# Retention of a hybrid layer in a hand-written order, one stream of weights, step sizes in eleven pieces, tiles at 64-byte starts

## The chip, the core and the metric

One core of one Trainium2 chip runs the whole layer as one program. The metric is the device time of one execution in microseconds (us). The kernel before takes 1260.97 us, the median of three executions (1256.4 to 1261.17).

## The reference: what is computed

A layer with 512 latent tokens, 256 context tokens and a model width of 1024 runs two branches side by side: retention (4 heads, keys of 256, values of 512) and a state-space scan (32 heads in 8 groups, state 128, chunks of 64 tokens). Both go forward and backward over the tokens, with the context first. A gated merge and a norm close the layer. Everything is float32.

```python
h_l = rmsnorm(x, norm_pre) * (1 + scale_l) + shift_l      # latent; h_c for the context
q, k, v, g, z, xbc, dt, gt = split(h @ w_in)              # both sequences
# retention, per head and direction: y_t = q_t h_t,  h_t = gamma h_{t-1} + k_t v_t^T
yr = bidir_scan(q, k, v, log_gamma)
# scan: depthwise conv of width 5 and silu on xbc -> xs, B, C; dt = softplus(dt + bias)
ys = bidir_scan(C, B, xs * dt, dt * A)
yr = (yr - mean(yr)) * rsqrt(var(yr) + EPS) * ret_gn_w    # per head
o_ret = (yr * silu(g)) @ w_ret_o
ys = groupnorm((ys + D * xs) * silu(z))
o_ssd = (ys * ssd_norm_w) @ w_ssd_o
out = (sigmoid(g_r) * o_ret + sigmoid(g_s) * o_ssd) @ w_out
x_new = x + gate * rmsnorm(out, norm_post)
```

## The kernel before, in words

Matmuls run on the fp32r type. To keep float32 accuracy each operand is split into a high part (`hh`, `whi`, `qh`, `vh`, `ah`) and a rest (`hl`, `wlo`, `ql`, `vl`, `al`), and each product takes three matmuls: high by high, high by rest, rest by high (`mm3`, L139 to L146; `v_unit`, L183 to L192). The high part is a cast on ScalarE and the rest a subtraction on VectorE. Weights come in units of 128 by 1024 values: a DMA into `wraw`, the cast (L134) and the subtraction (L135), with three buffers of each (`wunit`, L127).

The program has five stages.

1. Prologue, 0 to 60 us: the norm, the modulation, transposes of x, and head 0's q and k. It stands in an order written out by hand (`tc.manual_schedule()`), in which every engine takes its instructions as they are written.
2. Retention, 60 to 495 us, loop `for h in range(4)`: `strip` makes the decay table of a head (L579 to L585); `attention` (L588 to L617) does six steps of scores, decay, split and values: `a` is scores by decay on VectorE (L598), `ah` its cast on ScalarE (L162), `al` its rest on VectorE (L163), and then 12 matmuls into four accumulators (L608 to L610); `gproj` makes the gate (four weight units, L633); `norm` normalises the result into `yn` (L619); `qkv` makes the next head's q, k, v (eight weight units); `finish` (L645) turns `yn` with 16 transposes (L648), multiplies it with the gate into `u` (L650) and stores `u` in DRAM (L651). Apart from head 0's q, k and v, no order is written for this stage: a scheduler sets it when the program is built, from its own estimates.
3. `stepsizes` (L654 to L778), which the scan needs later, is written in the same loop as two pieces, the first behind head 1's q, k and v: a projection (L671), the softplus (`log1p_exp`, L167), sums along the tokens (L699 and L703), exponentials (L727 to L742), and eleven small DMAs that put the rows into DRAM and fetch a table back (L757 to L761); the second, behind head 2's q, k and v, is nine transposes and their copies (L766 to L776).
4. Scan, 495 to 1000 us: again an order by hand (`slot`), one weight unit to a slot.
5. Tail, 1000 to 1260 us: the output projections (L144 to L146 on `uh`, `ul`, and L1329) in the scheduler's order.

Tiles come from pools that place them one behind the other at 32-byte steps, from the left or from the right end of a partition. `vt` takes 1160 bytes, `nhalf` 4, `osq` 16, and so on, so that some pools' tiles start on a multiple of 64 bytes and others 32 bytes past one. On a multiple of 64 start `hh`, `hl`, the three buffers each of `wraw`, `whi` and `wlo`, all large tiles of retention, and, in the tail, the pool `f1` (it holds six of the eight pairs `uh`, `ul` of the second output projection). 32 bytes past one start the prologue's `xt`, `xn`, `wmod` and its fourth weight unit, the scan's `rows`, `x2`, `c2`, `st`, `vw`, `xtok`, `btok`, and, in the tail, the pools `fp` and `f2`: all eight pairs `uh`, `ul` of the first output projection, the other two of the second, and the operand `mg` of the last product (L1329).

Of the kernel before, what the change touches and what calls it, by code (L numbers as in the profile page):

```python
# [63 lines left out]

@with_exitstack
def hybrid_layer_kernel(ctx: ExitStack, tc: tile.TileContext, x, xc, vec, tab, msk, w_mod, bgate, npost,
# [4 lines left out]
    cp = ctx.enter_context(tc.tile_pool(name="cp", bufs=1))  # L71
    wp = ctx.enter_context(tc.tile_pool(name="wp", bufs=3))
# [51 lines left out]
    hp = hstack.enter_context(tc.tile_pool(name="hp", bufs=1))  # L124
# [57 lines left out]

    def v_unit(pv, u, wu, tiles=range(6)):  # L183
# [12 lines left out]
    with ExitStack() as st:  # L196
        p0 = st.enter_context(tc.tile_pool(name="p0", bufs=1))
        pw = st.enter_context(tc.tile_pool(name="pw", bufs=4))
        px = st.enter_context(tc.tile_pool(name="px", bufs=6))
        p2 = st.enter_context(tc.tile_pool(name="p2", bufs=2))  # L200
# [24 lines left out]
        srcs = [w_q[0], w_q[1], w_k[0], w_k[1]]  # L225
# [9 lines left out]
        def load_w(c):  # L235
            wraw[c] = (wp if c < 3 else p0).tile([P, UNIT], F32, name="wraw", tag="wraw")
            nc.sync.dma_start(wraw[c], srcs[c])
# [160 lines left out]
        vraw, vws = [], []  # L398

        def load_v():  # L400
            vraw.append(wp.tile([P, UNIT], F32, name="wraw", tag="wraw"))
            nc.sync.dma_start(vraw[-1], w_v[0, len(vraw) - 1])

        def cast_v():
            hi = wp.tile([P, UNIT], F32R, name="whi", tag="whi")
            nc.scalar.copy(hi, vraw[len(vws)])
            vws.append([hi])

        def rest_v():
            w, raw = vws[-1], vraw[len(vws) - 1]  # L410
            w.append(wp.tile([P, UNIT], F32R, name="wlo", tag="wlo"))
            nc.vector.tensor_tensor(w[1], raw, w[0].bitcast(F32), ALU.subtract)

        for _ in range(3):
            load_v()
        context = {5: (0,), 6: (1, 2)}
        select(3)
        for k in range(2, KT):
            acc(0, k)
            if k + 1 < KT:  # L420
                modulate(k + 1, context.get(k, ()))
            else:

                cast_v()
                head(3, 1)
                head(4, 1)
                rest_v()
                tail(3, 1)
                tail(4, 1)
# [22 lines left out]
        v_unit(first_v, 0, vws[0], range(2))  # L452
# [8 lines left out]
    with ExitStack() as st:  # L461
        rc = st.enter_context(tc.tile_pool(name="rc", bufs=1, reuse_waits="tile"))
        r1 = st.enter_context(tc.tile_pool(name="r1", bufs=1, reuse_waits="tile"))
        r2 = st.enter_context(tc.tile_pool(name="r2", bufs=2, reuse_waits="tile"))
# [64 lines left out]
        def first_qkv():  # L529
# [6 lines left out]
            load_v()  # L536
            read = [rope_read(accs[2 + c], c, *k_dst(c)[:2]) for c in range(2)]
            cast_v()
            rest_v()
# [6 lines left out]
            pv = first_v + [bank2() for _ in range(4)]  # L546
            for u in range(4):
                v_unit(pv, u, vws[u], range(6) if u else range(2, 6))
                if u < 2:
                    cast_v()  # L550
                    rest_v()
                if u == 1:
# [4 lines left out]
        def qkv(h):  # L557
            for c in range(2):
                ps = bank()
                proj(ps, projw(wunit(w_q[h * 2 + c])), 0, LT)  # L560
                rope(ps, c, q_dst(c))
            for c in range(2):
                wk = projw(wunit(w_k[h * 2 + c]))
# [3 lines left out]
                proj(pc, wk, LT, LC)  # L567
                rope(ps, c, k_dst(c))
                split(kh[:, c, LT:], kl[:, c, LT:], pc)

            pv = [bank() for _ in range(2)] + [bank2() for _ in range(4)]
            for u in range(4):
                v_unit(pv, u, wunit(w_v[h, u]))
            for i in range(6):
                split(vh[:, i, :], vl[:, i, :], pv[i])

        def strip(h):
# [8 lines left out]
            return e1, ec  # L586
# [46 lines left out]
        def gproj(h):  # L633
            g2 = big["g2"]
            for d in range(4):
                wk = projw(wunit(w_g[h * 4 + d]))
                ps = bank()
                proj(ps, wk, 0, LT)
                th = r2.tile([P, LT], F32, name="gth", tag="sw")
                nc.scalar.activation(th, ps, AF.Tanh, scale=0.5)  # L640
                nc.vector.scalar_tensor_tensor(g2[:, d, :], th, 1.0, ps, ALU.add, ALU.mult)
            return g2

        def finish(h, yn, g2):
            for d in range(4):  # L645
                ps = bank()
                for j in range(4):
                    nc.tensor.transpose(ps[:, j * P:(j + 1) * P], yn[:, j, d * P:(d + 1) * P], ident)  # L648
                u = r2.tile([P, LT], F32, name="u", tag="t1")
                nc.vector.scalar_tensor_tensor(u, ps, col(V_GN + h * 4 + d), g2[:, d, :], ALU.mult, ALU.mult)  # L650
                nc.sync.dma_start(u_d[0][h * 4 + d], u)  # L651

        def stepsizes():

            sp = st.enter_context(tc.tile_pool(name="sp", bufs=1))
            t = lambda n, w=384: sp.tile([P, w], F32, name=n, tag=n)

            raw = wp.tile([P, UNIT], F32, name="wraw", tag="wraw")
            nc.sync.dma_start(raw, w_dt)
            both = wp.tile([P, UNIT], F32R, name="whi", tag="whi")  # L660
# [146 lines left out]
        for h in range(4):  # L807
# [4 lines left out]
            if h < 3:  # L812
                qkv(h + 1)
# [645 lines left out]
```

## Time and profile before

| | |
|---|---|
| median of three executions | 1260.97 us |
| the profiled execution, its own time | 1262.49 us |
| its span, first to last instruction | 1260.7 us |
| mean granted TensorE clock | 0.994 of full speed |
| TensorE matmul (PE) busy | 1232.9 us, 6539 matmuls |
| VectorE (DVE), ScalarE (ACT), GpSimd (POOL) busy | 820.3, 440.4, 323.6 us |

PE's busy time comes from matmuls that overlap in the pipeline: one of 128 x 512 is recorded with 0.39 us, and the next one starts 0.227 us after it. How fast PE goes is therefore read from the distance of starts, or from the count of matmuls in a stretch, and lost time from gaps between starts.

### The profile page before, as it was taken

The page shows a single profiled execution, that of the slowest core. Times are in us where ns is not written, and L with a number is a line of the kernel's source. Part 1 is how long each engine was busy: PE and PEld are TensorE (multiplying, and loading weights), DVE is VectorE, ACT ScalarE, POOL GpSimd, SP SyncE. Part 2 cuts the span into 40 slices and gives each one's busy share as a digit, 9 for nine tenths or more (in the row PEclk, how much of TensorE's full clock was granted, in tenths as well). Part 3 has the DMA queues.
Part 4 walks back from the last instruction along what each step waited for, and adds up shares of the span by engine and source line. Part 5 has one row for each costly group of instructions (what it writes and reads, how often), then busy time and mean ns, then how long its engine had stood idle before and what let it go on. Part 6 is the DMA issues. An engine that isn't in the chain of part 4 may idle for free.

```text
span 1260.7 us, 16364 instructions
## 1 busy us (share of the span) xinstructions
PE 1232.9 (98%) x6539; PEld 1020.5 (81%) x6539; DVE 820.3 (65%) x971; ACT 440.4 (35%) x702; POOL 323.6 (26%) x267
## 2 busy tenths in 40 slices
PE   8999999899999999999999999999999999999997
PEld 6688887688888888888888888888878888888876
DVE  5576434853454253979999999999993357254533
ACT  4452323233323212444444434444442443122221
POOL 0021010001011000375565757565572200000000
PEclk9999999899999999999999999999999999999999
DMA  9330212122202214325253342515343567344621
GB/s 373 123 108 32 84 68 92 21 85 67 84 34 84 67 51 147 146 67 201 64 204 120 148 184 84 201 51 217 115 154 101 174 192 224 112 149 153 215 84 67
DMA packets 43101, 155.94 MB, mean 124 GB/s; under 512 B 5097, under 2 KB 5897, under 8 KB 37906
## 3 DMA queue, kind: packets, MB, share of 16 engines
q1 hardware_dynamic: 42322, 152.77, 34.8%
q0 software_dynamic: 704, 2.13, 0.7%
q8 instruction: 51, 0.84, 0.3%
q14 instruction: 24, 0.20, 0.0%
HBM read 144.10 MB, written 10.78 MB: 123 GB/s over the span
## 4 chain that ended last, share of the span: by engine, by line
PE 83%; DVE 12%; issue 3%; ACT 1%; DMA 1%; DVEq 0%; SPq 0%; POOLq 0%; ACTq 0%
PE pj L144 11%; PE pj L145 11%; PE pj L146 11%; PE pr L144 7%; PE pb L191 7%; PE pr L146 7%; PE pr L145 7%; PE pj L191 3%; PE py L1058 3%; DVE wlo L800 2%; PE pj L1329 2%; PE pb L1329 2%; PE tk L1005 2%; DVE cacc L887 2%; PE pb L610 2%
## 5 line engine op out<-in xcount | busy, mean ns | idle before, releaser
L144 PE MATMUL pr<-hh,whi 128*128 128x512 f32 (+1 forms) x640 | 240.9, 376 | 0.0
L146 PE MATMUL pr<-hh,wlo 128*128 128x512 f32 (+1 forms) x640 | 229.4, 358 | 0.0
L145 PE MATMUL pr<-hl,whi 128*128 128x512 f32 (+1 forms) x640 | 229.3, 358 | 0.0
L135 DVE TENSOR_TENSOR wlo<-wraw,whi 128x1024 fp32r<-128x1024 f32 x80 | 97.9, 1224 | 151.1 <-ACT whi L134 148.5
L134 ACT CAST whi<-wraw 128x1024 fp32r<-128x1024 f32 x80 | 84.3, 1053 | 229.9 <-PE pj L145 156.3
L144 PEld LDWEIGHTS pr<-hh,whi 128*128 128x128 f32 x640 | 121.0, 189 | 21.0 <-issue 4.6
L145 PEld LDWEIGHTS pr<-hl,whi 128*128 128x128 f32 x640 | 121.1, 189 | 18.1 <-issue 1.9
L146 PEld LDWEIGHTS pr<-hh,wlo 128*128 128x128 f32 x640 | 120.9, 189 | 18.0
L144 PE MATMUL pj<-hh,whi 128*128 128x512 f32 (+1 forms) x352 | 130.6, 371 | 0.0
L145 PE MATMUL pj<-hl,whi 128*128 128x512 f32 (+1 forms) x352 | 130.4, 370 | 0.0
L146 PE MATMUL pj<-hh,wlo 128*128 128x512 f32 (+1 forms) x352 | 130.4, 370 | 0.0
L1027 POOL TENSOR_TENSOR rows<-rows,ctok 128x512 f32<-128x512 f32 x64 | 92.3, 1467 | 104.8 <-DMA rows<-rows_d 104.8
L1044 POOL TENSOR_TENSOR rows<-c,rows 128x512 f32<-128x512 f32 x64 | 116.0, 1838 | 0.0
L800 DVE TENSOR_TENSOR wlo<-wraw,whi 128x1024 fp32r<-128x1024 f32 x56 | 91.5, 1633 | 20.9 <-ACT whi L793 20.9
L146 PE MATMUL pj<-uh,wlo 128*128 128x512 f32 x256 | 101.2, 395 | 0.0
L145 PE MATMUL pj<-ul,whi 128*128 128x512 f32 x256 | 100.8, 394 | 0.0
L144 PE MATMUL pj<-uh,whi 128*128 128x512 f32 x256 | 100.4, 392 | 0.0
L887 DVE SCALAR_TENSOR_TENSOR cacc<-raw,vt,cacc 128x772 f32<-128x772 f32 x48 | 74.8, 1559 | 14.6 <-ACT cacc L885 13.7
L896 ACT ACTIVATE cth<-cacc 128x772 f32<-128x772 f32 (+1 forms) x32 | 25.5, 796 | 145.1 <-DVE cacc L892 145.1
L144 PEld LDWEIGHTS pj<-hh,whi 128*128 128x128 f32 x352 | 66.3, 188 | 11.7 <-issue 0.2
L145 PEld LDWEIGHTS pj<-hl,whi 128*128 128x128 f32 x352 | 66.4, 189 | 11.3
L146 PEld LDWEIGHTS pj<-hh,wlo 128*128 128x128 f32 x352 | 66.3, 188 | 11.3
(303 smaller groups left out, 2316.8 us busy)
## 6 DMA issues: line engine op xcount, KB each, us to landing
rows<-rows_d SPq DMA_DIRECT2D x32, 1024.0 KB, 7.5
wmod<-in_w_mod_dram SPq DMA_DIRECT2D x8, 1024.0 KB, 10.9
wraw<-in_w_v_dram SPq DMA_DIRECT2D x16, 512.0 KB, 3.4
wraw<-in_w_g_dram SPq DMA_DIRECT2D x16, 512.0 KB
wraw<-in_w_xs_dram SPq DMA_DIRECT2D x16, 512.0 KB, 3.6
wraw<-in_w_z_dram SPq DMA_DIRECT2D x16, 512.0 KB, 3.4
wraw<-in_w_gt_dram SPq DMA_DIRECT2D x16, 512.0 KB, 4.6
uraw<-u_d SPq DMA_DIRECT2D x32, 256.0 KB, 3.7
```

The source lines that it names most:

```text
L134: nc.scalar.copy(hi, raw)
L135: (eng or nc.vector).tensor_tensor(lo, raw, hi.bitcast(F32), ALU.subtract)
L144: nc.tensor.matmul(ps, ah, bh, start=(first and i == 0), stop=False)
L145: nc.tensor.matmul(ps, ah, bl, start=False, stop=False)
L146: nc.tensor.matmul(ps, al, bh, start=False, stop=(last and i == n - 1))
L191: nc.tensor.matmul(pv[i], a[:, k, sl], wv[b][:, k2, :], start=(k == 0 and j == 0), stop=(k == KT - 1 and j == 2))
L800: nc.vector.tensor_tensor(lo, r, hi.bitcast(F32), ALU.subtract)
L887: nc.vector.scalar_tensor_tensor(acc, raw[:, i:i + n], col(w0 + i), acc, ALU.mult, ALU.add)
L1027: nc.gpsimd.tensor_tensor(v64(rows[:, d, :]), v64(rows[:, d, :]), bc(cb, 3, 64), ALU.add)
L1044: nc.gpsimd.tensor_tensor(rows[:, 2 + d, :], self.c2, rows[:, 2 + d, :], ALU.mult)
L1058: nc.tensor.matmul(py[64 * q:64 * q + 64, sl], lhs, rhs, start=(term == 0), stop=(term == 2))
L1329: nc.tensor.matmul(pss[e], mg[k][a][:, sl], wo[k][b][:, ec], start=(k == 0 and j == 0), stop=(k == KT - 1 and j == 2))
```

## The change

It has four parts.

- Retention is put under the hand-written order: `order.close()` moves from the end of the first q, k and v to the end of the scan, so that prologue, retention and scan are one order. The loop over heads is written out for it: `attention`, `norm`, then four gate units (`gate(d)`), with a quarter of the old `finish` (`turned(h, d)`, four transposes, one `u`, one store) behind the second, third and fourth unit and the last behind the first q unit; `strip(h + 1)` stands behind the first gate unit.
- All weight units from head 0's values to the scan's gates stand in one list `srcs`. `ahead()` casts and splits the unit two ahead, and `rest` loads the one three further.
- `stepsizes` gets nine more `yield`s: its first stage is eleven pieces, the first behind head 0's gate and the others one each behind a value unit or a gate unit (`step()`); its last, the nine transposes, stands at the end of head 3.
- `Lines` wraps the pools: a tile whose row isn't a multiple of 64 bytes is rounded up to one, `x2` rows get 784 instead of 772 values, and a tile `edge` of 32 bytes at the right end shifts everything that is placed from there.

What each engine computes is the same, instruction by instruction.

```diff
+class Lines:
+    def tile(self, shape, dt, **kw):
...
+        if n % 16 == 0:
+            return self.pool.tile(shape, dt, **kw)
+        t = self.pool.tile([shape[0], -(-n // 16) * 16], dt, **kw)[:, :n]
+        return t if len(shape) == 2 else t.rearrange("p (a b) -> p a b", a=shape[1])
...
-    cp = ctx.enter_context(tc.tile_pool(name="cp", bufs=1))
+    cp = Lines(ctx.enter_context(tc.tile_pool(name="cp", bufs=1)))
+    edge = ctx.enter_context(tc.tile_pool(name="edge", bufs=1, side="right"))
+    edge.tile([P, 8], F32, name="edge", tag="edge")
...
+    srcs = [w_v[0, u] for u in range(4)]
+    for h in range(4):
+        srcs += [w_g[h * 4 + d] for d in range(4)]
+        if h == 0:
+            srcs.append(w_dt)
+        if h < 3:
+            srcs += [w[h * 2 + 2 + c] for w in (w_q, w_k) for c in range(2)] + [w_v[h + 1, u] for u in range(4)]
...
+        def ahead():
+            cast(at[0] + 1)
+            rest(at[0] + 1)
+
+        def values(pv, first=False):
             for u in range(4):
-                v_unit(pv, u, vws[u], range(6) if u else range(2, 6))
...
+                v_unit(pv, u, unit(), range(2, 6) if first and u == 0 else range(6))
+                ahead()
+                if first and u == 1:
                     log_decays()
+                    strip(0)
+                if u < 3:
+                    step()
             for i in range(6):
                 split(vh[:, i, :], vl[:, i, :], pv[i])
...
-        def finish(h, yn, g2):
-            for d in range(4):
...
+        def turned(h, d):
+            ps = bank()
+            for j in range(4):
+                nc.tensor.transpose(ps[:, j * P:(j + 1) * P], big["yn"][:, j, d * P:(d + 1) * P], ident)
+            u = r2.tile([P, LT], F32, name="u", tag="t1")
+            nc.vector.scalar_tensor_tensor(u, ps, col(V_GN + h * 4 + d), big["g2"][:, d, :], ALU.mult, ALU.mult)
+            nc.sync.dma_start(u_d[0][h * 4 + d], u)
...
         first_qkv()
-        order.close()
-        steps = stepsizes()
         for h in range(4):
-            e1, ec = strip(h)
-            py = attention(h, e1, ec)
-            g2 = gproj(h)
-            yn = norm(py)
-            if h < 3:
-                qkv(h + 1)
-            if h < 2:
-                next(steps)
...
-            finish(h, yn, g2)
+            py = attention(h, stripe, ecs)
+            norm(py)
+            gate(0)
+            if h < 3:
+                strip(h + 1)
+            gate(1)
+            turned(h, 0)
+            step()
+            gate(2)
+            turned(h, 1)
+            step()
+            gate(3)
+            step()
+            if h == 0:
+                pieces[0] = 1
+                next(steps)
+            if h < 3:
+                turned(h, 2)
+                qkv(lambda: turned(h, 3))
+            else:
+                next(steps)
+                turned(h, 2)
+                turned(h, 3)
...
+        prev.early()
+        order.close()
```

How the instructions move shows best on VectorE where head 1's attention opens. Of before, from the first of the four `u` to the first score product (`dtu`, `dts`, `dt` belong to the step sizes, `wlo` is a weight's rest, `a` the scores by the decay):

```order
L650 SCALAR_TENSOR_TENSOR u<-pj,vt,g_706 128x512
L676 TENSOR_TENSOR dtu<-dtu,dtm 128x384
L650 SCALAR_TENSOR_TENSOR u<-pj,vt,g_706 128x512
L680 TENSOR_SCALAR dtu<-dtu,vt 128x384
L135 TENSOR_TENSOR wlo<-wraw,whi 128x1024
L169 TENSOR_SCALAR dts_1713<-dte 128x384
L650 SCALAR_TENSOR_TENSOR u<-pj,vt,g_706 128x512
L170 RECIPROCAL dts<-dts_1713 128x384
L650 SCALAR_TENSOR_TENSOR u<-pj,vt,g_706 128x512
L171 TENSOR_TENSOR dts<-dts,dte 128x384
L598 TENSOR_TENSOR a<-pj,strip 128x512
```

Of the change, the same place: the end of the step sizes' softplus, the last weights' rests, the six splits of the values, and the first score product:

```order
L196 TENSOR_SCALAR dt<-dt 128x384
L244 TENSOR_TENSOR wlo<-wraw,whi 128x1024
L740 TENSOR_TENSOR dt<-dt,dtu 128x384
L743 TENSOR_SCALAR dta<-dta 128x1
L745 TENSOR_SCALAR dtu<-dt,dta 128x384
L244 TENSOR_TENSOR wlo<-wraw,whi 128x1024
L182 TENSOR_TENSOR vl<-pj,vh 128x512 x2
L182 TENSOR_TENSOR vl<-pb,vh 128x512 x4
L661 TENSOR_TENSOR a<-pj,strip 128x512
L182 TENSOR_TENSOR al<-a,ah 128x512
```

The `u` and the step sizes no longer stand between the values' splits and the scores; they come before, among the projections.

On TensorE, before, head 0's 16 transposes stood together, between the step sizes' projection and head 1's scores:

```order
L671 MATMUL pj<-hh,whi 128x256
L671 MATMUL pj<-hl,whi 128x256
L648 MATMUL pj<-ident,yn 128x128 x16
L144 MATMUL pj<-qh,kh 128x512
L145 MATMUL pj<-ql,kh 128x512
```

Of the change, head 0's second group of four, between the third and the fourth gate unit (`whi`, `wlo` of the gate's weights):

```order
L164 MATMUL pj<-hl,whi 128x512
L165 MATMUL pj<-hh,wlo 128x512
L700 MATMUL pj<-ident,yn 128x128 x4
L163 MATMUL pj<-hh,whi 128x512
```

Each group of four now has a weight unit of 24 matmuls before it and, but for head 3's last two, one behind it. In prologue, scan and tail every engine keeps its order, but for one weight load that SyncE issues earlier at the prologue's end.

## Rows read from the trace of the kernel before

**Rows 1.** The page, part 1: busy us of each engine (share) xinstructions.

```profile
PE 1232.9 (98%) x6539; PEld 1020.5 (81%) x6539; DVE 820.3 (65%) x971; ACT 440.4 (35%) x702; POOL 323.6 (26%) x267
```

**Rows 2.** Windows, PE: start:end us, length, busy (xmatmuls), clock, DMA share, GB/s.

```profile
213.00:253.00 40.00, 32.20 (x119) 0.87 0.18 50
...
1035.00:1115.00 80.00, 80.00 (x345) 1.00 0.51 161
1122.00:1202.00 80.00, 80.00 (x351) 1.00 0.53 173
```

**Rows 3.** Waits of PE: engine line <- releaser: us in total, times, longest us.

```profile
PE pb L608 <- ACT ah L162: 4.6, 1, 4.6
PE tk L1005 <- DVE vw L990: 4.3, 7, 1.7
...
PE pj L648 <- DVE g L641: 1.2, 1, 1.2
```

**Rows 4.** Timeline, PE: start us, us, engine, line, operation, [idle before <-releaser].

```profile
217.61 0.50 PE L144 MATMUL pj<-qh,kh 128*128 128x512 f32 x1 [1.88 <-DVE u L650]
...
220.64 0.79 PE L144 MATMUL pj<-qh,kh 128*128 128x512 f32 x1 [0.87 <-DVE u L650]
221.23 0.63 PE L145 MATMUL pj<-ql,kh 128*128 128x512 f32 x1
221.66 0.63 PE L146 MATMUL pj<-qh,kl 128*128 128x512 f32 x1
...
248.57 0.51 PE L608 MATMUL pb<-vh,ah 128*128 128x512 f32 x1 [4.55 <-ACT ah L162]
...
340.91 0.98 PE L610 MATMUL pb<-vh,al 128*128 128x512 f32 x3 [0.84 <-DVE al L163]
```

**Rows 5.** Timeline, DVE, at the opening of head 1's attention.

```profile
217.47 2.54 DVE L170 RECIPROCAL dts<-dts 128x384 f32<-128x384 f32 x1
...
220.97 0.68 DVE L598 TENSOR_TENSOR a<-pj,strip 128x512 f32<-128x512 f32 x1
```

**Rows 6.** Timeline, DVE and ACT, at the opening of head 0's attention.

```profile
100.39 0.69 DVE L598 TENSOR_TENSOR a<-pj,strip 128x512 f32<-128x512 f32 x1
...
101.00 1.22 DVE L135 TENSOR_TENSOR wlo<-wraw,whi 128x1024 fp32r<-128x1024 f32 x1
...
101.12 0.62 ACT L162 CAST ah<-a 128x512 fp32r<-128x512 f32 x1 [0.56 <-DVE a L598]
...
102.13 0.69 DVE L163 TENSOR_TENSOR al<-a,ah 128x512 fp32r<-128x512 f32 x1
```

**Rows 7.** Chain of waits, a run of transposes: start us, us, what, count.

```profile
332.86 0.98 PE pj L766 x9
```

**Rows 8.** Groups by line, DVE, 205 to 262 us: busy us, mean ns.

```profile
L175 DVE SCALAR_TENSOR_TENSOR dt<-dt,dts 128x384 f32<-128x384 f32 x7 | 3.8, 549 | 0.0
...
L699 DVE TENSOR_TENSOR_SCAN cum<-dtm,dtu 32x384 f32<-32x384 f32 x2 | 1.9, 947 | 0.1
```

**Rows 9.** Tile tot_d: SyncE's issue, ns min/median/max; landing time of its DMAs.

```profile
L760 SPq DMA_DIRECT2D tot_d<-et x1: 582/582/582, 246.2 to 246.2; - x1
...
DMA to landing us min/median/max: 2.7/2.7/2.7
```

**Rows 10.** Chain of waits, runs of 128 x 512 matmuls.

```profile
77.22 5.44 PE pb L191 x24
...
1209.08 22.35 PE pb L1329 x96
1231.43 22.38 PE pj L1329 x96
```

**Rows 11.** Line L163: duration ns min/median/max, first and last start us.

```profile
L163 DVE TENSOR_TENSOR ul<-uraw,uh x40: 673/692/694, 992.3 to 1212.4; 128x512 fp32r<-128x512 f32 x40
...
L163 DVE TENSOR_TENSOR al<-a,ah x24: 678/692/1671, 102.1 to 465.8; 128x512 fp32r<-128x512 f32 x24
```

**Rows 12.** Window, all engines, the scan.

```profile
500.00:950.00 450.00, 445.54 (x2792) 376.05 (x2792) 419.25 (x390) 191.90 (x335) 267.12 (x190) 1.00 0.39 142
```

More of the change, by code (lines that the diff above doesn't have):

```diff
@@ L397, in hybrid_layer_kernel @@
         nc.sync.dma_start(tb, tab[:, 0:T_ID])
[L398 to L415, printed above, removed]
+        for t in range(3):
+            load(t)
         context = {5: (0,), 6: (1, 2)}
@@ L422, in hybrid_layer_kernel @@
             else:
-                cast_v()
+                cast(0)
                 head(3, 1)
                 head(4, 1)
-                rest_v()
+                rest(0)
                 tail(3, 1)
@@ L451, in hybrid_layer_kernel @@
         first_v = [bank(i=i) for i in (2, 3)]
-        v_unit(first_v, 0, vws[0], range(2))
+        v_unit(first_v, 0, wks[0], range(2))
         first_k = []
@@ L535, in first_qkv @@
                 rope_rest(read[c][0], *q_dst(c)[2:])
-            load_v()
             read = [rope_read(accs[2 + c], c, *k_dst(c)[:2]) for c in range(2)]
-            cast_v()
-            rest_v()
+            cast(1)
+            rest(1)
             for c in range(2):
@@ L567, in qkv @@
                 proj(pc, wk, LT, LC)
+                ahead()
                 rope(ps, c, k_dst(c))
                 split(kh[:, c, LT:], kl[:, c, LT:], pc)
[L571 to L575, printed above, removed]
+            values([bank() for _ in range(2)] + [bank2() for _ in range(4)])
         def strip(h):
@@ L653, in stepsizes, with gate @@
+        def gate(d):
+            ps = bank()
+            proj(ps, projw(unit()), 0, LT)
+            ahead()
+            th = r2.tile([P, LT], F32, name="gth", tag="sw")
+            nc.scalar.activation(th, ps, AF.Tanh, scale=0.5)
+            nc.vector.scalar_tensor_tensor(big["g2"][:, d, :], th, 1.0, ps, ALU.add, ALU.mult)
         def stepsizes():
-            sp = st.enter_context(tc.tile_pool(name="sp", bufs=1))
+            sp = Lines(st.enter_context(tc.tile_pool(name="sp", bufs=1)))
@@ L665, in stepsizes @@
+            ahead()
             u = t("dtu")
@@ new lines, in hybrid_layer_kernel @@
+        for i in range(4):
+            fetch(i)
+        jobs, dst = group_jobs(0)
+        prev = old = cur = None
+        t = scan0
+        for g in range(-1, 8):
+            nxt = Scan(g + 1, *dst) if g < 7 else None
+            for s, job in enumerate(jobs):
+                held = prev if g == 7 and s == 1 else None
+                if held:
+                    prev = Late(prev)
+                slot(s, t, job, prev, old, cur, nxt)
+                if held:
+                    sbx.close()
+                    fr = Lines(fstack.enter_context(tc.tile_pool(name="fr", bufs=1, side="right", reuse_waits="tile")))
+                    gr = fr.tile([P, KT, LT], F32, name="gr", tag="gr")
+                    for d in range(KT):
+                        jobs[d].dst = gr[:, d, :]
+                    held.early()
+                prev = job
+                t += 1
+            old, cur = cur, nxt
+            if g < 6:
+                jobs, dst = group_jobs(g + 2)
+            else:
+                jobs = [Gate(w_gt[d], None, False) for d in range(KT)]
```

195 lines of the change are left out of this document (87 added, 108 removed).

## The prediction

> **What bounds the kernel now.** I read the page first: TensorE's matmul row is busy for 98% of the span, and no other engine for more than 65% [rows 1]. So the chain that sets the end runs through PE, and time can come from two places only: gaps between matmuls, and matmuls that follow each other more slowly than they could. The busy figure shows neither, since a matmul of 512 columns is recorded with 0.39 us while its follower starts sooner. So next I read counts. Where nothing disturbs, 24 matmuls take 5.44 us, which is 0.2267 us each [rows 10]; this is the pace that everything below is held against.
>
> For the gaps I went to the windows of PE and to its waits. In the 40 us from 213 to 253 only 119 matmuls begin, at a mean granted clock of 0.87 [rows 2]; at the pace it would be 176. So 57 x 0.2267 = 13.0 us are lost there. The timeline shows three things in it [rows 4]: two waits of 1.88 and 0.87 us for `u`, one of 4.55 us for `ah`, and, behind the idle stretches, matmuls 0.43 us apart (221.23 to 221.66) instead of 0.23. [...] DVE's timeline shows why `u` and `ah` are late: the step sizes' reciprocal of 2.54 us starts at 217.47 among the four `u`, and the first `a` of the attention only at 220.97 [rows 5]. Two smaller gaps follow: 0.84 us for `al` at head 2 [rows 4] and 1.2 us in which head 3's transposes wait for a gate [rows 3]. Everything else of retention runs at the pace.
>
> **The change, part by part.**
>
> *The old gaps.* With the fixed order, no `u` and no step-size operation stands between the values' splits and the attention's products. The 13.0 us go, and with them the low clock, since PE no longer stands idle before those matmuls. The two small gaps go too: 13.0 + 0.8 + 1.2 = **15.0 us**.
>
> *What the fixed order costs instead.* At the opening of each attention PE has only two score blocks (12 matmuls, 2.72 us) ahead of the first product. In head 0, which has this order already but for one `wlo` of 1.22 us, `a` starts at 100.39, `ah` ends at 101.74 [rows 6]. PE is through its scores by about then. Without the `wlo`, `al` would follow at once and end 0.69 us later, at 102.43; the order now wants it as third matmul, at 101.74 + 2 x 0.2267 = 102.19. That is 0.24 us a head, **1.0 us** for four; the bounds are nothing (the scheduler's order hid it) and 0.84 us a head, the row of head 2 [rows 4], 3.4 in all. In the later steps the same chain, 0.69 + 0.62 + 0.69 = 2.0 us, runs beside the step before it, 12 matmuls or 2.72 us, and is covered. At head 3's end the third `u` needs the bank of the last gate, whose cast and product take about as long as one `ah` and one `a`, 1.3 us [rows 6], against nine transposes of 0.98 us that stand between [rows 7]: **0.4 us**, from nothing to the 1.2 of the row that it replaces [rows 3]. Twelve more groups of transposes change no count; the bound is a switch of 0.1 us each, 1.2 in all, and I take nothing, since the nine at 332.86 follow fp32r matmuls and still take 0.109 us each [rows 7].
>
> *The step sizes in eleven pieces* keep their instructions; I cost them at nothing, because of what covers them. The longest piece is the softplus: one reciprocal of 2.54 [rows 5] and 13 operations of at most 0.55 [rows 8], under 9.7 us on DVE. It stands behind a value unit of 36 matmuls, 8.2 us of PE, and DVE also owes that unit's `wlo` of 1.22 us. DVE falls behind by some 3 us. It may: the rests are made two units ahead, and the next pieces (the sums, two pairs of 0.95 us [rows 8], and shorter ones) are smaller than their units. Without that lead it would cost those 3 us once. Their eleven DMAs pass SyncE's queue behind head 2's second gate, at 0.58 us or less each, plus one wait of 2.7 us for a landing [rows 9], at most 9 us. Weight loads queue behind them, but each is issued three units, 16 us, before its cast. If that lead were gone the price would be those 9 us, once. The loads, stores and POOL's work are spread, not added.
>
> *Tiles at 64-byte starts.* In the tail, 384 matmuls of the first output projection stream tiles that start 32 bytes past a 64-byte line, and they go at 80/345 = 0.2319 us [rows 2]; in the second, where twelve of sixteen operands start on a line, it is 80/351 = 0.2279 us [rows 2]; the last 192 matmuls have one operand on a line and one off it, and take (22.35 + 22.38)/192 = 0.2330 us [rows 10]. PE is not waiting in any of them. Brought to the pace, this is 384 x 0.0052 + 384 x 0.0012 + 192 x 0.0063 = 2.0 + 0.5 + 1.2 = **3.7 us**. Bounds: nothing, if something else in the tail slows them, and 4.5 with the prologue's one such weight unit and rounding of the counts. [...] I follow the rows, because two projections of the same code, in the same stage, differ in nothing that I can see but the starts of their operands. For DVE I take nothing: the subtraction of 128 x 512 takes 692 ns on `uraw`, off the line, and 692 ns on `a`, on it [rows 11].
>
> *The sum*: 15.0 - 1.0 - 0.4 + 3.7 = 17.3 us less. The profiled execution's own time, 1262.49 us, becomes 1245.2. It stood 1.5 us above the median of the three runs, so the median is forecast at **1243.5 us**. About 0.5%, 6 us, is what a measurement of this kernel can tell from no change.
>
> **The rivals.**
>
> *The starts give nothing* (0.12). The tail's slow pace would then come from its traffic: its DMAs are busy at 0.51 and 0.53 [rows 2]. Against it, the two stretches have the same traffic and different paces. Time: 1243.5 + 3.7 = 1247.
>
> *The scan moves as well* (0.11). There DVE is busy 419 of 450 us, and PE waits for it 4.3 us in all at `vw` [rows 12, 3]. A scan that starts in another phase, or with `rows`, `st` and `x2` on a line, may lose or double these waits: 1239 or 1248.
>
> *The gaps only move* (0.06): the change doesn't do what it says, PE meets 13.6 us of new waits in the order by hand, and only the starts count: 1260.97 - 3.7 = 1257. Head 0's opening, in this order and without such gaps, speaks against it [rows 6].
>
> *Slower* (0.03). Each of the 24 attention steps has those 2.72 us of cover for its chain of 2.0 us. If POOL's work falls into that chain, `a` and `al` grow: the longest `al` is 1671 ns against 692 [rows 11]. With 0.98 us more for both, the chain is 4.0 us and PE waits 1.2 us a step, 24 x 1.2 = 30: 1273. It decides from 0.7 us of added time a step. [...] Against the rival: the new order gives POOL nothing to do during attention.
>
> **How the numbers follow.** The forecast has 0.68, with its own range of 1239 to 1247 from the bounds of its small terms. The range 1237 to 1251 takes in the starts and the scan, and the upper bounds of the openings. Faster by over 0.5% (below 1254.7): 0.68 + 0.12 + 0.11 = 0.91; within: 0.06; slower: 0.03.
>
> **What would show it.** Right: no stretch of retention with a clock below 1.0; projections and values at 0.227 us a matmul without gaps; PE's waits for `u` gone, four waits for `al` of some 0.25 us; both output projections and the last product at 0.227 us; the scan as long as before. Wrong: PE waiting for a `wlo` in head 1's values, or for `al` by over 1 us a head, or the tail still at 0.232.

## The result, and the profile after

The changed kernel takes 1244.86 us (median of four executions, 1244.13 to 1246.43); the kernel before, run beside it, 1259.43. The ratio is 0.989, with a 95% interval of 0.986 to 0.991. The profiled execution took 1245.43 us, its span is 1243.7. The forecast was 1243.5 with a range of 1237 to 1251, and on the profiled execution's scale 1245.2. By the medians the change gives 14.6 us. By the two profiled executions, from which the account below is cut, it gives 17.1, since the profiled execution of the kernel before, 1262.49, lies 3.1 us above its median.

The page of the kernel after, parts 1 and 4 (the busy shares, and who holds the chain that ended last):

```profile
PE 1224.3 (98%) x6539; PEld 1016.3 (82%) x6539; DVE 817.1 (66%) x971; ACT 439.4 (35%) x702; POOL 327.6 (26%) x267
...
PE 91%; DVE 6%; issue 2%; ACT 1%; DMA 1%; SPq 0%; DVEq 0%; POOLq 0%; ACTq 0%
```

PE's 98% is what it was [rows 1], which once more tells nothing. The windows tell it (start:end, length, PE busy (xmatmuls), clock, DMA share, GB/s):

```profile
212.00:252.00 40.00, 39.92 (x177) 1.00 0.04 14
1020.00:1100.00 80.00, 80.00 (x355) 1.00 0.53 163
1107.00:1187.00 80.00, 80.00 (x355) 1.00 0.55 182
```

Against [rows 2]: at head 1's opening 177 matmuls begin where there were 119, at the full clock; both output projections show 355 in 80 us, where there were 345 and 351. PE's waits (engine line <- releaser: us in total, times, longest), of which the two for `u` [rows 4] and the long one for `ah` [rows 3] are gone:

```profile
PE tk L1059 <- DVE vw L1044: 5.1, 6, 3.1
...
PE pj L700 <- DVE g L711: 0.4, 1, 0.4
```

The first of these grew, from 4.3 in all and 1.7 at most [rows 3]. Cutting the span at the starts of named matmuls (the first scores of head 0, the scan's first projection, each tail product) gives the account:

| stage, us | before | after | difference | forecast |
|---|---|---|---|---|
| start and prologue | 98.82 | 97.37 | -1.45 | 0 |
| retention | 395.68 | 383.07 | -12.61 | -13.6 |
| scan, with the gates behind it | 534.99 | 536.77 | +1.78 | 0 |
| first output projection | 89.61 | 87.04 | -2.57 | -2.0 |
| second output projection | 89.42 | 88.35 | -1.07 | -0.5 |
| last product | 44.88 | 43.74 | -1.14 | -1.2 |
| behind PE's last matmul | 7.32 | 7.32 | 0 | 0 |
| span | 1260.72 | 1243.66 | -17.06 | -17.3 |

The sum fits better than its terms, and that is luck. Retention gave 1.0 less than forecast, the tail 1.1 more, and a prologue and a scan that the change hardly touches moved by -1.5 and +1.8. The prologue's move is within its spread: it took 97.4 to 100.6 us in the fourteen profiled executions of this case.

Where retention lost is at the openings. PE's timeline at head 1's (start, us, operation), and below it DVE's and ACT's:

```profile
214.20 0.39 PE L164 MATMUL pj<-ql,kh 128*128 128x512 f32 x1
214.43 0.39 PE L165 MATMUL pj<-qh,kl 128*128 128x512 f32 x1
214.89 0.50 PE L671 MATMUL pb<-vh,ah 128*128 128x512 f32 x1
215.23 0.39 PE L672 MATMUL pb<-vl,ah 128*128 128x512 f32 x1
215.62 0.50 PE L673 MATMUL pb<-vh,al 128*128 128x512 f32 x1
215.95 0.39 PE L671 MATMUL pb<-vh,ah 128*128 128x512 f32 x1
...
213.49 0.69 DVE L661 TENSOR_TENSOR a<-pj,strip 128x512 f32<-128x512 f32 x1
...
214.87 0.69 DVE L182 TENSOR_TENSOR al<-a,ah 128x512 fp32r<-128x512 f32 x1 [0.69 <-ACT ah L181]
...
214.22 0.62 ACT L181 CAST ah<-a 128x512 fp32r<-128x512 f32 x1 [1.50 <-DVE a L661]
```

Matmuls at the pace start 0.227 us apart. Here the steps are 0.46, 0.34, 0.39 and 0.33, which is 0.61 us too much. PE waits for `ah`, which ends at 214.84, and two matmuls on for `al`, which ends at 215.56; and behind each of these two short waits the next start is 0.11 us late as well. The same four steps stand at all four heads: 4 x 0.61 = 2.5 us, where the forecast had 1.0. PE's own list of waits doesn't have them. They show in the distance of starts, and in the list of the weight loads (PEld, the loads of the held operand): there four waits for `ah` come to 2.0 us and four for `al` to 1.7.

The last product, in the chain of waits (start, us, what, count), answers to [rows 10], 22.35 and 22.38:

```profile
1193.16 21.80 PE pb L1383 x96
1214.97 21.77 PE pj L1383 x96
```

### The profile page after: what moved, and what is told of

Read it like the earlier page. It is cut to its first block, busy times and chain, and to the rows that moved or that the text cites. A ratio compares the mean times of both kernels' runs of the same rounds, so it can differ in the third digit from the quotient of the medians.

```text
span 1243.7 us, 16318 instructions
## 1 busy us (share of the span) xinstructions
PE 1224.3 (98%) x6539; PEld 1016.3 (82%) x6539; DVE 817.1 (66%) x971; ACT 439.4 (35%) x702; POOL 327.6 (26%) x267
## 4 chain that ended last, share of the span: by engine, by line
PE 91%; DVE 6%; issue 2%; ACT 1%; DMA 1%; SPq 0%; DVEq 0%; POOLq 0%; ACTq 0%
PE pj L165 11%; PE pj L163 11%; PE pj L164 11%; PE pr L163 9%; PE pr L164 9%; PE pr L165 9%; PE pb L257 7%; PE pj L257 4%; PE py L1112 3%; PE pb L673 2%; PE pb L671 2%; PE tk L1059 2%; PE pb L672 2%; PE pb L1383 2%; PE pj L1383 2%
## 5 line engine op out<-in xcount | busy, mean ns | idle before, releaser
L163 PE MATMUL pr<-hh,whi 128*128 128x512 f32 (+1 forms) x640 | 241.4, 377 | 0.0
L244 DVE TENSOR_TENSOR wlo<-wraw,whi 128x1024 fp32r<-128x1024 f32 x100 | 144.8, 1448 | 71.5 <-ACT whi L233 71.0
L163 PEld LDWEIGHTS pr<-hh,whi 128*128 128x128 f32 x640 | 121.3, 190 | 21.1 <-issue 4.7
L163 PE MATMUL pj<-hh,whi 128*128 128x512 f32 (+1 forms) x352 | 131.9, 375 | 0.0
L233 ACT CAST whi<-wraw 128x1024 fp32r<-128x1024 f32 x100 | 104.7, 1048 | 55.3 <-PE pb L257 49.3
L163 PE MATMUL pj<-uh,whi 128*128 128x512 f32 x256 | 99.6, 389 | 0.0
L154 DVE TENSOR_TENSOR wlo<-wraw,whi 128x1024 fp32r<-128x1024 f32 x40 | 49.0, 1224 | 43.6 <-ACT whi L153 43.6
L163 PEld LDWEIGHTS pj<-hh,whi 128*128 128x128 f32 x352 | 66.4, 189 | 11.2
```

The source lines that it names most:

```text
L154: (eng or nc.vector).tensor_tensor(lo, raw, hi.bitcast(F32), ALU.subtract)
L163: nc.tensor.matmul(ps, ah, bh, start=(first and i == 0), stop=False)
L233: nc.scalar.copy(wks[t], raw[t])
L244: nc.vector.tensor_tensor(lo, raw[t], hi.bitcast(F32), ALU.subtract)
```

## The experiments

Two questions were open. Which part of the change gave what, and by which mechanism? And is the scan's +1.8 us the change's doing? The stages of every run are cut as above, from its profiled execution. Five runs are one execution each: all tiles moved, only the weights moved, the offsets by steps, the padding of 64 bytes, and the block of ten pieces.

### The two parts alone

The order without the new starts:

```diff
     def tile(self, shape, dt, **kw):
-        n = 1
...
+        return self.pool.tile(shape, dt, **kw)
-    edge.tile([P, 8], F32, name="edge", tag="edge")
-            x2 = sg.tile([P, 2, 784], F32, name="x2", tag="x2")[:, :, 0:CONVW]
+            x2 = sg.tile([P, 2, CONVW], F32, name="x2", tag="x2")
```

> The order, the stream of weights and the eleven pieces of the change, but every tile placed as in the kernel before (no rounding up, no edge tile, x2 rows of 772). If the starts are what made the tail faster, its three stretches are back at 89.6, 89.4 and 44.9 us (first, second output projection, last product) and the time is 1244.9 + 4.8 = 1249.7 us. Rival, the starts give nothing and the tail gained from the order before it: 87.0, 88.4 and 43.7 us, and 1245 us in all. The scan, which grew from 535.0 to 536.8 us: if the order lengthened it, it is 536.8 here; if the new places of its tiles did, 535.0.

Measured: 1250.44 us (before beside it 1261.91; ratio 0.992, 0.989 to 0.995). Retention 383.36, scan 534.55, tail 89.62, 89.41 and 44.89. The tail's windows:

```profile
1020.00:1100.00 80.00, 80.00 (x345) 1.00 0.51 157
1110.00:1190.00 80.00, 80.00 (x350) 1.00 0.53 177
```

And the starts without the order, which is the same edit made to the kernel before:

> The kernel before with nothing changed but the places of the tiles (all at 64-byte starts). If the starts act alone and the parts add up: the tail at 87.0, 88.4 and 43.7 us, retention still 395.7 us with its gaps at head 1's opening, 1259.4 - 4.8 = 1254.6 us. Rival, the starts give nothing: the tail at 89.6, 89.4 and 44.9 us and 1259.4 us. The scan: 535.0 us if the order is what lengthened it, 536.8 if the places of its tiles did.

Measured: 1254.98 us (ratio 0.995, 0.992 to 0.997); the profiled execution is the shortest of the six, 1249.42. Retention 391.97 with the wait of 4.6 us for `ah` still there, scan 531.50, tail 87.04, 88.35 and 43.74, and its windows:

```profile
1024.00:1104.00 80.00, 80.00 (x355) 1.00 0.56 168
1111.00:1191.00 80.00, 80.00 (x355) 1.00 0.53 177
```

So the tail's gain belongs to the starts alone, to a hundredth of a microsecond. Retention's gain is there without the starts (383.36 against 383.07 with them), so it belongs to the other parts. But in the old order this execution's retention is 3.7 us shorter than that of the kernel before: the two waits for `u` come to 1.8 us, not 2.7, and from 205 to 228 us, around them, the granted clock is 1.00, where it was 0.85. No run separates whether that is the starts or a difference between executions of one order. The rival in which the starts give nothing is out. The two ratios multiply to 0.987, beside 0.989 for both together. The scan follows neither: it is 534.99 us with neither part, 534.55 with the order alone, 531.50 with the starts alone and 536.77 with both.

### What it is about the starts

Every tile moved 32 bytes past a multiple of 64:

```diff
-    edge = ctx.enter_context(tc.tile_pool(name="edge", bufs=1, side="right"))
-    edge.tile([P, 8], F32, name="edge", tag="edge")
+    off = ctx.enter_context(tc.tile_pool(name="off", bufs=1))
+    off.tile([P, 8], F32, name="off", tag="off")
     cp = Lines(ctx.enter_context(tc.tile_pool(name="cp", bufs=1)))
```

> The changed kernel with every tile of the left side moved by 32 bytes and the tile at the right end left out: all tiles start 32 bytes past a multiple of 64, both operands of every matmul alike. Theory A, the start itself counts: matmuls of 512 columns take 0.231 to 0.234 us instead of 0.2267 everywhere, the first output projection 89 us, the whole 1260 us or more (some 3,700 such matmuls x 0.005 = 19 us). Theory B, what counts is that the two operands of a matmul lie alike: all at 0.2267, the tail's stretches at 87.0, 88.4 and 43.7 us, 1245 us.

Measured: 1243.0 us, tail 87.04, 88.35 and 43.74: theory B. With no tile on a 64-byte multiple the kernel is as fast as with all of them there.

```profile
1017.00:1097.00 80.00, 80.00 (x354) 1.00 0.54 168
1104.00:1184.00 80.00, 80.00 (x354) 1.00 0.54 179
```

Only the weight units moved by 32 bytes (a tile of 32 bytes ahead of their pool and one behind it):

> The changed kernel with only the weight units (their raw, high and rest buffers) moved to 32 bytes past a multiple of 64. They are the held operand in the projections and the streamed one in the values. Theory A, the start of the streamed operand counts: projections stay at 0.2267 us a matmul (first output projection 87.0 us), the values' matmuls go to 0.231 to 0.234: 3 us more in all, 1248 us. Theory B, the two operands must lie alike: both slow, the output projections at 89 us each, 1260 us or more. Theory C, the start of the held operand counts as well as that of the streamed one: the same as B here, told from it by the run with all tiles moved.

Measured: 1259.06 us. The first output projection took 89.59 us, and the values, in which the weights are the streamed operand, 5.60 us for 24 (the chain of waits: start, us, what, count) where the kernel after has 5.44:

```profile
77.25 5.60 PE pb L261 x24
85.65 5.60 PE pb L261 x24
...
1206.26 22.03 PE pb L1387 x96
```

Theory A would keep the projections at the pace, and they aren't. With the run before it, this settles that neither operand's own start counts: what counts is whether the streamed and the held operand lie alike. The last row is a hint at more. In this run the last product's operands all start on multiples of 64, but those in one pool lie 64 bytes further from those in the other than in the kernel after, and 96 matmuls take 22.03 us there and not 21.80.

The offsets by steps:

```diff
+        o = (0, 1, 2, 4, 8, 12, 15, 16)[i]
+        ts = [pool.tile([P, 2 * LT + 16], F32R, name=f"{n}{i}", tag=f"{n}{i}")[:, o:o + 2 * LT] for n in ("uh", "ul")]
```

> The changed kernel with the eight pairs of streamed tiles of the first output projection started 0, 4, 8, 16, 32, 48, 60 and 64 bytes past a multiple of 64, read pair by pair (48 matmuls to a pair). Theory, the grain is 64 bytes: pairs 1 and 8 at 0.2267 us, all six others slow, at some 0.232 us. Rival, a grain of 16 bytes: the offsets 16, 32 and 48 also at 0.2267, only 4, 8 and 60 slow. The whole grows by at most 6 x 48 x 0.006 = 1.7 us and some in the later products, 1245 to 1248 us.

Measured: 1248.38 us, the projection 89.32. Sorted by the tiles' addresses, the mean distance of starts was 235 ns at 4 bytes, 232 at 8, 234 at 16, 232 at 32, 233 at 48, 230 at 60, and also 232 for the two pairs at 0 and 64. Neither reading holds: there is no sign of a grain of 16 bytes, but multiples of 64 didn't keep the pace either. Nor can the pairs be read one by one. In the second projection of the kernel before, six pairs lie alike with the weights and two don't; behind those two, the first of the six goes at 231.5 ns, the second at 228.3, and only the other four at 226.7. A pair that is off slows the next pair or two, and here nearly every pair stands behind one that is off. The padding of 64 bytes to each tile had also moved whole tiles against each other by multiples of 64. One more run asked about that alone:

```diff
+        ts = [pool.tile([P, 2 * LT + w], F32R, name=f"{n}{i}", tag=f"{n}{i}")[:, 0:2 * LT] for n, w in (("uh", 16), ("ul", 0))]
```

> The changed kernel with 64 bytes of padding behind each high tile of the eight pairs of the first output projection: every tile still starts on a multiple of 64, but their starts, measured from the held weights', run through all eight multiples of 64 within 512 bytes. Theory, a grain of 64 bytes: all eight classes at 0.2267 us a matmul, the projection 87.0 us, 1245 us. Rival, a coarser grain (the changed kernel itself has distances of 0 and 256 bytes within 512 there, and nothing between): the classes off 0 and 256 at 0.229 to 0.232 us, the projection 88.0 to 88.6 us; with a grain of 128 bytes the classes 128 and 384 stay at 0.2267, with 256 they are slow as well.

Measured: 1251.72 us, the projection 89.06, all eight classes slow, 230 to 234 ns a matmul, those at 0 and 256 with 234 too. In the second projection of the same run, where pairs 1 to 6 aren't padded, the first of those, behind the padded pairs, went at 232 ns, the last four at 226.7, and the operands at 320 and 384 bytes at 232. So a start on a multiple of 64 isn't enough. In the tail of the kernel after, by the places that the pools give (no trace has addresses), nearly all distances are 0 or 256 bytes within 512, and there they go at the pace. Where distances differ from one matmul to the next, even those at 0 are slow. What the grain is, and why a neighbour matters, stays open.

### What made the old gaps

The scheduler's order for retention, with all else of the change kept:

```diff
         first_qkv()
+        order.close()
         for h in range(4):
...
+        scanned = ExitStack()
+        scanned.enter_context(tc.manual_schedule())
         for i in range(4):
             fetch(i)
```

> The changed kernel, but the order by hand ends behind the first q, k and v and starts again at the scan, as in the kernel before; for retention the scheduler sets the order, with the eleven pieces, the stream of weights and the 64-byte starts kept. Theory, the fixed order is what took the gaps away: PE waits by over 1 us again for u, ah or a weight somewhere in retention, and the time is 1249 to 1258 us. Rival, it was the step sizes in one block that pushed u and a back, and small pieces are enough in any order: no wait over 1 us, 1244 to 1247 us.

Measured: 1246.14 us (ratio 0.988, 0.985 to 0.990); retention 381.99, which is 1.1 less than with the fixed order. At the openings 0.1 us a head is left: the scheduler puts 13 score matmuls ahead of the first product and five products with `ah` ahead of the first with `al`, the fixed order 12 and two. The largest waits are at head 3's end:

```profile
PE pj L700 <- ACT wtok L834: 0.8, 1, 0.8
...
PE pj L700 <- DVE g L711: 0.3, 1, 0.3
```

The rival holds. The fixed order isn't what took the gaps away. What remains is the places of the step sizes and of the `u` in the program, and the one stream of weights, which this run keeps and no run takes back. In the kernel before, none of PE's listed waits in retention is for a weight, which speaks against the stream but doesn't settle it. Two more runs put one of the two places back, both in the scheduler's order. First the step sizes, in one block with their projection behind head 1's values (`w_dt` behind `w_v` in `srcs`, eleven `next(steps)` behind `qkv`):

> As the run with the scheduler's order, but the step sizes stand in one block behind head 1's values again, projection first, as in the kernel before; the quarters of the gate's product stay spread. If the place of the step sizes made the 13 us gap at head 1's attention, it comes back: PE waits for ah by 3 us or more there, 1254 to 1260 us. If it was the four u behind the values, nothing comes back: 1246 us.

Measured: 1250.09 us (ratio 0.992, 0.989 to 0.995), retention 386.92, 4.9 more than with the pieces. But the loss is not at the opening. VectorE is still at the step sizes' sums when head 1's attention ends, reaches `yn` late, and PE waits there, and for one `al`:

```profile
PE pj L700 <- DVE yn L693: 2.6, 4, 1.5
...
PE pb L673 <- DVE al L182: 0.5, 1, 0.5
```

The kernel before lost most at nearly the same time. Its wait of 4.55 us for `ah`, at 248.57 [rows 4], is not at the opening either, but at the last of the six steps. VectorE's timeline, head 1's last `a` behind the step sizes' sums:

```profile
243.38 0.16 DVE L704 COPY tot<-cum 32x6 f32<-32x6 f32 x1
...
246.65 0.56 DVE L733 TENSOR_TENSOR rest<-tot,cum 128x384 f32<-128x384 f32 x1
247.13 0.68 DVE L598 TENSOR_TENSOR a<-pj,ec 128x512 f32<-128x512 f32 x1
```

PE's last matmul ahead of the gap starts at 243.63, and this `a` only at 247.13. So the same step sizes stand ahead of an `a` there and of `yn` here.

Then the 16 transposes and four `u` together behind the next head's values, with the step sizes early:

```diff
-            turned(h, 0)
...
-                qkv(lambda: turned(h, 3))
+                qkv(lambda: None)
...
+            for d in range(4):
+                turned(h, d)
```

> As the run with the scheduler's order, step sizes in pieces, but the 16 transposes and the four u of a head stand together behind the next head's values again, as in the kernel before. If the u made the gap, PE waits for u before the scores of heads 1 to 3, by 1 to 3 us a head: 1249 to 1256 us. If the step sizes alone made it, 1246 us.

Measured: 1249.64 us (ratio 0.991, 0.988 to 0.994), retention 385.97, 4.0 more. PE waits not for `u` but for the `al` that stands behind them, once at each of heads 1 to 3, and for `u` at the end:

```profile
PE pb L673 <- DVE al L182: 2.9, 3, 1.0
...
PE pr L163 <- DVE u L702: 1.3, 1, 1.3
```

4.9 + 4.0 = 8.9 us. Retention of before is 13.7 us longer than the scheduler's version of the change, and that of the run with the starts alone, in the same old order, 10.0 longer. So 1.1 to 4.8 us are left; the 3.7 between the two are shorter waits for `u` and the low clock around them (0.85 against 1.00). That the rest needs step sizes and `u` at one opening is not shown, since no run puts both back.

The last run on this has the fixed order, and the ten pieces behind the projection in one block behind head 1's first value unit (`while` for `if` in `step`):

> The changed kernel with the order by hand, but the step sizes' ten pieces after the projection run in one block behind head 1's first value unit. Their VectorE work of some 20 us then stands before the next unit's rest, which is needed two units, 16 us, later. If that lead is all that covers them: one wait of PE for a wlo of 5 to 15 us in head 1's values, with the low clock behind it, 1251 to 1262 us. Rival, the scheduler-like spread isn't needed, since PE has slack there: no such wait, 1245 us.

Measured: 1258.05 us, retention 394.76: 11.7 us lost. The timeline of PE, DVE and ACT:

```profile
205.39 0.39 PE L257 MATMUL pb<-whi,hl 128*128 128x512 f32 x1
210.75 0.79 PE L257 MATMUL pj<-whi,hh 128*128 128x512 f32 x1 [4.97 <-ACT whi L233]
215.04 0.79 PE L257 MATMUL pj<-wlo,hh 128*128 128x512 f32 x1 [3.50 <-DVE wlo L244]
215.64 0.63 PE L257 MATMUL pj<-whi,hl 128*128 128x512 f32 x1
...
213.76 3.50 DVE L244 TENSOR_TENSOR wlo<-wraw,whi 128x1024 fp32r<-128x1024 f32 x3
...
206.06 1.28 ACT L802 ACT_TABLE_LOAD   x1 [1.06 <-DVE dt L801]
...
207.95 1.28 ACT L804 ACT_TABLE_LOAD   x1
...
209.67 2.92 ACT L233 CAST whi<-wraw 128x1024 fp32r<-128x1024 f32 x3
```

PE stands for a weight's high part first: ScalarE's casts stand in its queue behind the step sizes' exponentials and logarithms, which wait for VectorE and load two tables of 1.28 us. Then it stands for the rest, 3.50 us, and goes on with starts 0.43 us apart (215.64 to 216.06 and on), as the kernel before did where its granted clock was 0.50 (221.23 to 221.66 [rows 4]; 0.50 from 219 to 224 us). The lead of two units is not enough for the block, and is for the pieces. The expectation had the length right and the first wait wrong: it named `wlo`, and the longer wait, 5.0 us, is for `whi`.

### Beyond both kernels

Three score blocks ahead of an attention's first product:

```diff
             scores(0)
+            scores(1)
             for i in range(6):
-                if i < 5:
-                    scores(i + 1)
+                if i < 4:
+                    scores(i + 2)
                 av(i)
```

> The changed kernel with three score blocks ahead of an attention's first product instead of two: 18 matmuls, 4.08 us, for the chain of a, ah and al that now ends 0.6 us late at each of the four openings. Theory, the openings lose only this: 4 x 0.63 = 2.5 us go, no wait for ah or al is left there, 1242.4 us. Rival, the buffers: ah and al have two, so the third block's cast waits for the first product, and PE waits for it at the third product instead; then the time stays at 1245 or grows by up to 1 us a head, 1249.

Measured: 1242.82 us (ratio 0.986, 0.983 to 0.988), retention 380.43, 2.6 less than after. The rival's wait at the third product isn't there. The opening of head 1 goes at the pace, from the last score to the third product:

```profile
216.75 0.39 PE L165 MATMUL pj<-qh,kl 128*128 128x512 f32 x1
216.98 0.39 PE L671 MATMUL pb<-vh,ah 128*128 128x512 f32 x1
217.21 0.39 PE L672 MATMUL pb<-vl,ah 128*128 128x512 f32 x1
217.44 0.39 PE L673 MATMUL pb<-vh,al 128*128 128x512 f32 x1
```

Next the scan's longest wait. The kernel after, VectorE and PE ahead of the last group:

```profile
913.78 3.31 DVE L1085 COPY_PREDICATED rows<-maskL,rows 128x512 f32<-128x512 uint32 x2
917.00 2.28 DVE L244 TENSOR_TENSOR wlo<-wraw,whi 128x1024 fp32r<-128x1024 f32 x1
...
919.80 0.74 DVE L1044 TENSOR_TENSOR vw<-tk,wtok 128x256 f32<-128x256 f32 x2
...
912.25 2.52 POOL L1081 TENSOR_TENSOR rows<-rows,ctok 128x512 f32<-128x512 f32 x2
914.74 3.45 POOL L1098 TENSOR_TENSOR rows<-c,rows 128x512 f32<-128x512 f32 x2
...
920.26 2.08 PE L1059 MATMUL tk<-vw,btok 128*128 128x256 f32 x4 [3.11 <-DVE vw L1044]
```

The two copies and the `wlo` run beside POOL's work, and the `wlo` takes 2.28 us and not its 1.22 [rows 6]. `vw`, which PE needs, stands behind them all. Behind the wait, from 921 to 923 us, the granted clock is 0.50. So, on top of the third block:

```diff
-                call(cur, ("turned", 0, 3), ("scores",))
+                call(cur, ("turned", 0, 3), ("choose", 0), ("choose", 1), ("scores",))
...
-                call(nxt, ("exponents", 3), ("choose", 0), ("choose", 1))
+                call(nxt, ("exponents", 3))
```

> The kernel with three score blocks ahead, and in the scan the two products vw that PE waits for (five or six times by 0.4 to 0.7 us, and by 3.1 to 3.3 us before the last group) are put ahead of the two predicated copies on VectorE, which nothing on PE waits for so soon. Theory, the waits are VectorE's queue and nothing else: they shrink to nothing, 3.3 + 5 x 0.5 us go and the low clock of some 1.8 us behind the longest one, 7 us: about 1236 us. Rival 1, VectorE as a whole is the bound of the scan: the wait only moves to a later product, 1243 us. Rival 2, the copies now come too late for the outputs: a new wait there, 1243 us or more.

Measured: 1237.38 us (1236.92 to 1237.74; ratio 0.982, 0.979 to 0.984), the fastest of all, and its four executions lie within 0.8 us. The scan is 529.78 us, 4.95 less than with the third block alone, and one wait is left:

```profile
911.00 0.74 DVE L1045 TENSOR_TENSOR vw<-tk,wtok 128x256 f32<-128x256 f32 x2
911.67 3.96 DVE L1086 COPY_PREDICATED rows<-maskL,rows 128x512 f32<-128x512 uint32 x3
```

```profile
PE tk L1060 <- DVE vw L1045: 0.8, 1, 0.8
```

The wait was a matter of the order in VectorE's queue. It was 5.4 us by the medians and not the 7 expected: 0.8 moved to a later `vw`, as the first rival has it, and the waits of the third block's kernel were 3.9 us in all, not 5.8.

This also answers the scan's +1.8. Leave out this run and the one with the weights moved; then there are twelve profiled executions, before and after among them, with one and the same order of the scan. It took 531.5 to 533.5 us in the four where `vw` cost PE 1.5 to 2.8 us in all, and 534.6 to 537.4 in the eight where it cost 3.9 to 5.1. Both kinds occur with the retention of before and with that of the change. Before and after are both of the longer kind, and their 1.8 us lie within its spread. With the old starts there are only two executions, both of the longer kind, so whether the starts have a share in it stays open, and so does what puts an execution into one kind or the other.

## Why the prediction was right, and where it was wrong

**What bounds the kernel, the old gaps (15.0).** Right in place and nearly in size: all of them are gone, and the 12.6 us that retention gained, with the 2.5 and 0.6 of new losses below, make 15.7. Wrong in one clause, "with the fixed order": the scheduler's order loses them as well. Wrong in one reading, too: `ah` was not late because the first `a` starts at 220.97 [rows 5]. The 4.55 us are at the last step, behind the step sizes' sums. And the low clock was taken as a part of the 13.0 that every execution has. In the kernel before it stands behind PE's two idle stretches (0.57 from 218 to 226 us and from 249 to 253, 1.00 in the rest of retention); but the run with the starts alone had none of it around its waits for `u`, 1.8 us in all (1.00 from 205 to 228), so that a wait brings it each time was not shown.

**The openings (1.0).** The mis-sized term: 2.5 measured. The chain from `a` to the end of `al` was right (2.07 us against 2.04). But PE was through its scores 1.17 us after `a` started, not the 1.35 at which `ah` ends, so it waits for `ah` too; and behind each short wait 0.1 us more goes. The prediction took PE's arrival from head 0 of the kernel before, which "has this order already". On PE it hasn't: 13 score matmuls stand there ahead of the first product, not 12, which is 0.23 us. The upper bound of 3.4 held it. The third score block took 2.6 us back, which shows that this term was these waits.

**Head 3's end (0.4).** Right: the wait for the gate is 0.4 us, PE's start 0.59 late.

**The groups of transposes (0).** Right. Of the switch of 0.1 us that was the bound the kernel after shows 0.08: the second matmul behind a group of four starts 0.31 us after the first and not 0.227 (157.03, 157.34). But the four take 0.36 us (156.67 to 157.03), so a group costs 0.44 us, 0.11 a transpose, as the nine do [rows 7].

**The step sizes (0).** Right for the pieces: none of PE's listed waits in retention is for a weight. The price of 3 us without the lead was not measured: the run with one block keeps the lead and puts ten pieces ahead of it, not one, which cost 11.7 us. It shows what the prediction left out: it counted VectorE's work alone, and ScalarE's casts queue behind the same chain.

**64-byte starts (3.7).** Right in place, too low in size (4.78), and wrong in its mechanism. Size: a window counts matmuls that are still running when it opens. At 0.39 us each and one each 0.23 us that is nearly two too many, so 80/345 gives 0.2319 us, where 384 in 89.61 us are 0.2334. Mechanism: not a start off a line, but two operands that lie differently; all tiles 32 bytes off are as fast (87.04 us for the 384). How far alike they must lie is open. The rival in which the starts give nothing fell with the first two runs: the places of the tiles alone made the 4.78 us.

**The scan moves (rival, 0.11).** It did, by +1.8, but in the way in which it moves between executions of other kernels too.

**Slower (0.03), gaps only move (0.06).** Neither came: no `a` or `al` of an attention waits for POOL, and the 24 `al` take 691 to 696 ns. In the kernel before, the six `al` that overlap POOL's `ec` (L585) took 1.18 to 1.67 us and the others 0.68 to 0.69; why they grow was not shown.

## What to carry over

Ask of each engine's queue what stands ahead of the operation that PE waits for next: moving side work (step sizes, predicated copies) behind it or into a slack place was worth 4 to 12 us here, in a fixed order and in a scheduler's alike. When matmuls without waits run a few per cent under the pace (0.233 us against 0.227 here), compare the start addresses of the two operands with each other, not each with a line, and keep their distance the same from one matmul to the next. Read a pace from runs of the chain or from starts, not from counts in a window, and look for short waits in the distance of starts and among the weight loads' waits, since the matmuls' own list didn't have them here. Look at where a wait stands before naming what it waits behind: the longest one was 24 us past the opening that it was put down to.

## What the runs showed of the hardware

- A 128 x 512 matmul starts 0.2267 us after the last one when both operands lie alike, on a multiple of 64 bytes (first output projection of the kernel after) or 32 past one (all tiles moved), and 0.2333 us after it when one of them lies 32 bytes off the other (kernel before, only the weights moved). Where the distance changes from pair to pair it is 0.230 to 0.235 us (the offsets by steps), even if all starts are multiples of 64 (the padding of 64 bytes, 0.230 to 0.234).
- Two pairs that are off slow the next two: 0.2315 and 0.2283 us, then 0.2267 (second projection of the kernel before).
- Behind waits of 0.24 and 0.16 us PE's next start is 0.11 us late (kernel after, head 1's opening).
- In one and the same order of instructions the granted clock from 205 to 228 us was 0.85 in one execution (the kernel before) and 1.00 in another (the starts alone).
- On ScalarE, the logarithm and the exponential that follow each other in the step sizes load a table of 1.28 us each (206.06 and 207.95, the block of ten pieces).
- Executions of one kernel differ by up to 7.9 us (the kernel before, 1256.4 to 1264.31 beside the run with `vw` first; 1249.42 to 1256.75 with the starts alone); with `vw` ahead of the copies four lay within 0.8.
